# Opening attention's pool ahead of the layer norm's last steps, with its stores and key loads on GpSimd's queue, in a fused hybrid encoder layer

## The chip, the cores and the metric

The kernel runs on one core of one Trainium2 chip. The metric is the device time of one execution in microseconds (us). All times below are of the kernel before the change.

## The reference

One layer over 2048 tokens of width 1024, in float32, with a batch of one:

```python
mod = c_act @ w_ada + b_ada                       # adaptive norm
shift, scale, gate = split(mod, 3)
h = rmsnorm(x, norm_w) * (1 + scale) + shift
proj = h @ w_in + b_in                            # 1024 -> 4624 columns
na_q, na_k, na_v, na_z, ml_q, ml_k, ml_v, ml_o, ml_z, gates = split(proj)
na = neighbourhood_attention(na_q, na_k, na_v, rpb) * silu(na_z)
                                                  # 8 heads of 64, an 8 x 16 window on a 32 x 64 grid
mq, mk = split(silu(short_conv([ml_q, ml_k])))
hm = mlstm(mq, mk, ml_v, fwd gates) + flip(mlstm(flipped, bwd gates))   # 4 heads of 128
ml = layer_norm(hm * sigmoid(ml_o)) * ml_norm_w * silu(ml_z)
x = x + gate * (concat(na, ml) @ w_out)
out = rmsnorm(x) * final_norm_w
```

## The kernel before

Every product of activations and weights is done as three matmuls on high and low parts (`hhi`, `hlo`, `whi`, `wlo`) that add into one PSUM tile. The normalised input stays in SBUF, transposed, in four groups of 512 tokens (`hhi0` to `hhi3` and `hlo0` to `hlo3`).

**Phase 1** makes the values, gates, the mLSTM's queries and keys, the tables of the attention's bias and the output weights times the gate, and parks most of them in DRAM.

**Phase 1b** (from about 555 us) runs the mLSTM head by head: `ml_pass1` builds the states chunk by chunk, `ml_pass2` makes the outputs and their moments, and a queue of small closures (`normalise`, `turn`, `end`, store) finishes the layer norm a few steps behind. `close_step` pops these queues. The product `hm` times the output gate of each chunk is GpSimd's, and VectorE's `bn_stats` reads what it leaves. Between these small steps TensorE is fed from the generator `nq_gen`, which makes the remaining projections: mLSTM's gate (`mz`), attention's gate (`nz`), keys (`k`) and queries (`q`). `pump(n)` puts n of its matmuls into the program. A turn of `nq_gen` is one strip of 128 weight columns: `nq_load` reads it to a single buffer (`rawq`), `nq_split` makes `whi` on ScalarE and `wlo` on GpSimd, or on VectorE for the queries, and 24 matmuls go to each group of tokens. ScalarE copies the result to `qst` as the high part, VectorE makes the low part in the same tile, and both go to DRAM (`d_kna`, `d_qna`). For keys and queries these two stores wait in the list `late` until the next group's third step. There are two such tiles, used in turn.

When the groups 3 and 2 are no longer needed as inputs their buffers become the keys of the attention, `kk`: the second half of the tokens is read back by the 16 loads of `kk_jobs`, each queued by `job` inside `close_step`; the first half is written there directly.

**Phase 2** does the attention in 16 patches of 8 x 16 tokens, four units (pairs of heads) each. `slot(n)` is written out by hand (`manual_schedule`): scores of unit n (`stage_s`: queries `qhigh` and `qlow`, a bias table `tab`, VectorE adds and takes the minimum, ScalarE takes the exponential into `pbuf`), outputs of n-2, transposes of n-1, loads, and a number of pumped matmuls. The slots 0 to 4 pump what is left of the queries' projection, 22 matmuls a slot; the later ones pump the output projection.

**Between the two** stands the end of the mLSTM: after its last step a loop runs `close_step` and `pump(PUMP3)` until the norm's queues are empty, then the pools `ml` (SBUF) and `ms` (PSUM) close, and `phase2` opens its pool `p2` in their place. A tile of the new pool waits for the last use of the old tiles at its address. The last gate tile, `zt_last`, stands in the ring of the `ck` tiles of `ml`, and its store is the last thing that the old pool does.

SyncE's, ScalarE's and GpSimd's instruction streams each issue DMAs in their own order. The framework also keeps eight semaphores for the DMAs that SyncE and ScalarE issue and eight for those of GpSimd; a DMA waits until the one that last used its semaphore has landed.

Of the kernel before, what the change touches and what calls it, by code (L numbers as in the profile page):

```python
# [58 lines left out]
class Kernel:  # L59
# [780 lines left out]
    def nq_gen(self):  # L840
# [10 lines left out]
        for i, s, g in order:  # L851
# [6 lines left out]
            for k in range(KT):  # L858
                w1, w2 = whi[:, k, off : off + P], wlo[:, k, off : off + P]
                for n, (w, h) in enumerate(((w1, self.hhi), (w1, self.hlo), (w2, self.hhi))):  # L860
                    nc.tensor.matmul(patch_ps(ps) if patch else ps, w, self.htok(h, g, k, patch), start=(k == 0 and n == 0), stop=(k == KT - 1 and n == 2))  # L861
# [48 lines left out]
        while late:  # L910
            nc.scalar.dma_start(*late.pop(0))
# [15 lines left out]
    def phase1b(self, left, right):  # L927
        nc = self.nc
        mls = ExitStack()
        ml = self.pool(mls, "ml", bufs=1, side="right")  # L930
        pps, pss = ExitStack(), ExitStack()
        self.pp = self.pool(pps, "pp2", bufs=2, space=PSUM)
        self.ms = self.pool(pss, "ms", bufs=1, space=PSUM)
# [4 lines left out]
        self.perm = ml.tile([P, P], F32, name="perm")  # L938
# [10 lines left out]
        for j, (steps, cur) in enumerate(passes):  # L949
            nxt = passes[j + 1][1] if j + 1 < len(passes) else iter(())  # L950
            for i in range(steps):
                if i in (steps - 4, steps - 1):
                    next(nxt, None)
                next(cur)
        while self.norms or self.turns or self.ends or self.stores:
            self.close_step()
            self.pump(PUMP3)
        mls.close()
        pss.close()
        self.todo = []  # L960
        self.stacks = [pps, right, left]
# [5 lines left out]
    def kk_jobs(self):  # L967
# [77 lines left out]
    def ml_pass2(self, ml, h):  # L1045
# [11 lines left out]
        def load_z(gi):  # L1057
            while ("mz", h, gi) not in self.zdone:
                self.pump(1)
            if h == MH - 1 and gi == NG - 1:  # L1060
                t = ml.tile([P, 769], F32, tag="ck", bufs=4, name="zt_last")[:, :512].rearrange("p (a q) -> p a q", a=4)
            else:
                t = ml.tile([P, 4, CH], F32, tag="zt", bufs=1, name=f"zt_{h}_{gi}")
# [12 lines left out]
        def combine(c):  # L1076
# [23 lines left out]
            if c % 4 == 0:  # L1100
                hm[gi] = ml.tile([P, 4, CH], F32, tag="hm", bufs=2, name=f"hm_{h}_{gi}")
                mv[gi] = ml.tile([P, 4, 2], F32, tag="mv", bufs=2, name=f"mv_{h}_{gi}")
# [5 lines left out]
        def moments(c):  # L1108
            gi = c // 4
            b6 = ml.tile([P, 6], F32, tag="b6", bufs=2, name=f"b6_{h}_{c}")  # L1110
            nc.vector.bn_stats(b6, hm[gi][:, c % 4, :])
            nc.vector.bn_aggr(mv[gi][:, c % 4, :], b6)
            if c % 4 == 3:
                v = ml.tile([P, 4], F32, tag="var", bufs=2, name=f"var_{h}_{gi}")
                y = ml.tile([P, 4], F32, tag="rstd", bufs=2, name=f"rstd_{h}_{gi}")
                nc.vector.tensor_scalar(v, mv[gi][:, :, 1], EPS, None, ALU.add)
                self.rsqrt(ml, y, v, f"{h}_{gi}")
                mu = ml.tile([P, 4], F32, tag="mu", bufs=2, name=f"mu_{h}_{gi}")
# [38 lines left out]
        for c in range(NC):  # L1157
# [37 lines left out]
    def phase2(self):  # L1195
# [426 lines left out]
```

## Time and profile before

| | |
|---|---|
| Median of 3 runs | 1409.82 us (1407.24 to 1413.92) |
| Profiled execution | 1409.69 us, of which the span is 1407.8 us |
| TensorE busy | 1316.7 us, 94% of the span |
| VectorE, ScalarE, GpSimd busy | 834.7, 529.7, 284.5 us |
| Bytes of DMA | 264.73 MB, 188 GB/s in the mean |
| Mean granted TensorE clock | 0.983 |

The profile is of one execution. "busy" of TensorE has the pipelined ends of matmuls in it. A row of the timeline gives start and length in us, the engine, the line, the operation with its tiles, and in brackets the idle time just before it with what ended that. A name such as ACTq or SPq is an engine's issuing of a DMA; its length is that of the issue and not of the transfer. A row that ends in "x4" holds four instructions merged. The windows view gives the busy time of each engine in a stretch, then the granted TensorE clock and the busy share of the DMA engines.

### The profile page before, as it was taken

The page shows a single profiled execution, that of the slowest core. Times are in us where ns is not written, and L with a number is a line of the kernel's source. Part 1 is how long each engine was busy: PE and PEld are TensorE (multiplying, and loading weights), DVE is VectorE, ACT ScalarE, POOL GpSimd, SP SyncE. Part 2 cuts the span into 40 slices and gives each one's busy share as a digit, 9 for nine tenths or more (in the row PEclk, how much of TensorE's full clock was granted, in tenths as well). Part 3 has the DMA queues.
Part 4 walks back from the last instruction along what each step waited for, and adds up shares of the span by engine and source line. Part 5 has one row for each costly group of instructions (what it writes and reads, how often), then busy time and mean ns, then how long its engine had stood idle before and what let it go on. Part 6 is the DMA issues. An engine that isn't in the chain of part 4 may idle for free. (4 is left out here: it accounts for less than half of the span.)

```text
span 1407.8 us, 23381 instructions
## 1 busy us (share of the span) xinstructions
PE 1316.7 (94%) x8052; PEld 1127.7 (80%) x8052; DVE 834.7 (59%) x2565; ACT 529.7 (38%) x1131; POOL 284.5 (20%) x309
## 2 busy tenths in 40 slices
PE   3989998898999999999999998999989999999996
PEld 2889998888887787788878786788867888888885
DVE  6683423211355569156757777877637777777674
ACT  4642344523222323113323313323336555555551
POOL 4353221424101010001212002212112211112111
PEclk9999999999999999999999999999999999999998
DMA  9798448777467675555666777946598897776862
GB/s 319 225 297 202 121 125 213 190 184 204 117 116 208 143 186 163 161 166 150 196 190 212 238 225 214 232 127 180 145 275 223 197 222 169 197 192 173 190 159 75
DMA packets 273036, 264.73 MB, mean 188 GB/s; under 512 B 33498, under 2 KB 233818, under 8 KB 272918
## 3 DMA queue, kind: packets, MB, share of 16 engines
q1 hardware_dynamic: 181486, 187.17, 50.3%
q0 software_dynamic: 21408, 38.05, 11.0%
q10 hardware_dynamic: 70024, 38.02, 9.6%
q8 instruction: 64, 1.05, 0.3%
q14 instruction: 54, 0.44, 0.1%
HBM read 178.62 MB, written 92.72 MB: 193 GB/s over the span
## 5 line engine op out<-in xcount | busy, mean ns | idle before, releaser
L861 PE MATMUL pq<-hhi,whi_a 128*128 128x512 f32 x512 | 211.6, 413 | 0.8 <-ACT u L769 0.8
L861 PE MATMUL pq<-hhi,wlo_a 128*128 128x512 f32 x512 | 211.4, 413 | 0.3 <-DVE wlo_a L838 0.3
L861 PE MATMUL pq<-hlo,whi_a 128*128 128x512 f32 x512 | 211.3, 413 | 0.0
L1342 ACT ACTIVATE pbuf<-pbuf,mn 128x480 f32<-128x480 f32 (+5 forms) x128 | 76.4, 598 | 115.3 <-DVE mn L1341 108.9
L861 PEld LDWEIGHTS pq<-hhi,whi_a 128*128 128x128 f32 x512 | 98.3, 192 | 19.4 <-ACT u L769 1.2
L861 PEld LDWEIGHTS pq<-hhi,wlo_a 128*128 128x128 f32 x512 | 98.2, 192 | 19.0 <-DVE wlo_a L838 0.8
L861 PEld LDWEIGHTS pq<-hlo,whi_a 128*128 128x128 f32 x512 | 98.3, 192 | 17.9
L1341 DVE CUSTOM_DVE_ANT_0 pbuf<-pS,tab 128x480 f32<-128x480 f32 (+5 forms) x128 | 65.2, 541 | 37.3 <-DMA tab<-d_t 20.1
L1415 PE MATMUL y<-hhi,whi_a 128*128 128x512 f32 x256 | 84.7, 400 | 0.7 <-ACT whi_a L1388 0.7
L1415 PE MATMUL y<-hhi,wlo_a 128*128 128x512 f32 x256 | 84.3, 399 | 0.0
L835 POOL TENSOR_TENSOR wlo_a<-rawq,whi_a 128x1024 fp32r<-128x1024 f32 x20 | 48.3, 2417 | 167.0 <-ACT whi_a L834 52.4
L425 PE MATMUL pvo<-whi_b,hhi 128*128 128x256 f32 x256 | 74.7, 292 | 7.5 <-DVE stvo L495 7.5
L1106 POOL TENSOR_TENSOR hm<-hm,ck 128x128 f32<-128x128 f32 x64 | 26.4, 413 | 266.5 <-DVE hm L1105 190.7
L1087 ACT ACTIVATE num<-px,gtile 128x129 f32<-128x129 f32 x120 | 38.2, 364 | 96.8 <-PE px L1082 79.9
L426 PE MATMUL pvo<-wlo_b,hhi 128*128 128x256 f32 x256 | 73.7, 288 | 0.0
L427 PE MATMUL pvo<-whi_b,hlo 128*128 128x256 f32 x256 | 73.5, 287 | 0.0
L1014 DVE TENSOR_SCALAR wv<-kv,gtile 128x129 f32<-128x129 f32 x120 | 38.5, 328 | 58.4 <-PE dc L1030 30.4
L495 DVE TENSOR_TENSOR stvo<-pvo,brow 128x256 f32<-128x256 f32 x64 | 26.6, 421 | 73.4 <-PE pvo L427 59.5
L710 ACT ACTIVATE dec<-dec,gtile 128x128 f32<-128x128 f32 x128 | 42.1, 392 | 74.0 <-POOL dec L706 64.8
L460 DVE TENSOR_TENSOR stv<-pv,brow 128x256 f32<-128x256 f32 x32 | 12.5, 421 | 89.2 <-DMA d_vna<-stv 41.6
L1363 PE MATMUL pT<-ident,pbuf 128*128 128x128 f32 (+2 forms) x416 | 59.8, 283 | 2.8 <-DVE pbuf L1353 2.8
L1378 PE MATMUL pO<-pt,v 128*64 128x128 f32 (+3 forms) x832 | 61.0, 280 | 1.3 <-ACT pt L1365 0.8
(295 smaller groups left out, 3578.0 us busy)
## 6 DMA issues: line engine op xcount, KB each, us to landing
ck<-d_ck SPq DMA_DIRECT2D x64, 384.5 KB
kv<-d_ck SPq DMA_DIRECT2D x120, 128.5 KB
rawq<-in_w_main_dram SPq DMA_DIRECT2D x30, 512.0 KB
raw<-in_w_main_dram SPq DMA_DIRECT2D x20, 512.0 KB
d_ck<-stvo SPq DMA_DIRECT2D x16, 514.0 KB
x<-in_x_dram SPq DMA_DIRECT2D x16, 512.0 KB
wada<-in_w_ada_dram SPq DMA_DIRECT2D x32, 256.0 KB
dec<-d_mneg SPq DMA_DIRECT2D x32, 256.0 KB
```

Of the source, the lines that this page charges most:

```text
L425: nc.tensor.matmul(ps, lhi(k), rhi(k), start=(k == 0), stop=False)
L426: nc.tensor.matmul(ps, lhi(k), rlo(k), start=False, stop=False)
L427: nc.tensor.matmul(ps, llo(k), rhi(k), start=False, stop=(k == KT - 1))
L710: nc.scalar.activation(t[:, d, o, :], t[:, d, o, :], AF.Exp, bias=self.cols["g"][:, d, h, c : c + 1])
L835: nc.gpsimd.tensor_tensor(lo[:, :, cs], raw, hi[:, :, cs].bitcast(F32), ALU.subtract)
L861: nc.tensor.matmul(patch_ps(ps) if patch else ps, w, self.htok(h, g, k, patch), start=(k == 0 and n == 0), stop=(k == KT - 1 and n == 2))
L1014: nc.vector.tensor_scalar(wv, tiles[d, i][:, 128:257], self.cols["w"][:, d, h, c : c + 1], None, ALU.mult)
L1341: nc.vector.tensor_tensor_reduce(pt[:, :nk], ps, tabs[place[u]][j][:, :nk], 1.0, 3e38, ALU.add, ALU.min, mn)
L1342: nc.scalar.activation(pt[:, :nk], pt[:, :nk], AF.Exp, bias=mn, scale=-1.0, accum_out=sums[:, j : j + 1])
L1363: nc.tensor.transpose(ps[:cs, i, :], pts[j][:, i * cs : (i + 1) * cs], self.ident)
L1378: nc.tensor.matmul(po[j * HD : (j + 1) * HD, :], v[:n, h * HD : (h + 1) * HD], pt[j][:n, i, :], start=(i == 0), stop=(i == nch - 1))
L1415: nc.tensor.matmul(y, m[:, k, :], w[k][:, cs], start=(k == 4 and n == 0), stop=(k == 3 and n == 2))
```

## The change

Four things are done at once. The layer norm's closing tiles (`zt`, `hm`, `mv`, the moments, `perm`) get a pool of their own, `mle`, that lies outside `ml` and lives on through phase 2, so that `ml` closes before the closing loop. The loop itself moves to a method `close`, called from `phase2` after `p2` is open and the first loads of the attention stand in the program; the last `load_z` moves there too, and `zt_last` becomes a tile of `p2`. The PSUM pools of phase 2 still open after the loop. Small tiles of phase 2 and three of the four `pbuf` take the places of closed norm tiles in `mle`. The late stores of keys and queries go from ScalarE's queue to GpSimd's, the 16 key loads from SyncE's to GpSimd's, the first six `qlow` loads from SyncE's to GpSimd's, and four of the eight loads of output weights from GpSimd's to SyncE's.

```diff
@@ nq_gen (here and at its end)
                         while late:
-                            nc.scalar.dma_start(*late.pop(0))
+                            nc.gpsimd.dma_start(*late.pop(0))
@@ phase1b
+        self.mle = self.pool(right, "mle", bufs=1, side="right")
         mls = ExitStack()
         ml = self.pool(mls, "ml", bufs=1, side="right")
...
-        while self.norms or self.turns or self.ends or self.stores:
-            self.close_step()
-            self.pump(PUMP3)
         mls.close()
-        pss.close()
         self.todo = []
         self.stacks = [pps, right, left]
+
+    def close(self):
+
+        self.last_z()
+        while self.norms or self.turns or self.ends or self.stores:
+            self.close_step()
+            self.pump(PUMP3)
+        self.pss.close()
@@ kk_jobs
-            self.nc.sync.dma_start(self.kk[ct][row : row + HD, j * T + T // 2 : (j + 1) * T].bitcast(F32), src)
+            self.nc.gpsimd.dma_start(self.kk[ct][row : row + HD, j * T + T // 2 : (j + 1) * T].bitcast(F32), src)
@@ ml_pass2 (zt, hm, mv, b6, var, rstd, mu: ml becomes self.mle)
             if h == MH - 1 and gi == NG - 1:
-                t = ml.tile([P, 769], F32, tag="ck", bufs=4, name="zt_last")[:, :512].rearrange("p (a q) -> p a q", a=4)
+                t = self.p2.tile([P, 4, P], F32, tag="pt", bufs=2, name="zt_last")
...
-                if h == MH - 1:
-                    load_z(NG - 1)
+                self.last_z = lambda: load_z(NG - 1)
@@ phase2
-        p = self.pool(rgt, "p2", bufs=1, side="right")
-        pss = ExitStack()
-        pS = self.pool(pss, "pS", bufs=3, space=PSUM)
-        pT = self.pool(pss, "pT", bufs=2, space=PSUM)
-        pO = self.pool(pss, "pO", bufs=1, space=PSUM)
+        p = self.p2 = self.pool(rgt, "p2", bufs=1, side="right")
+        few = self.mle
...
-                nc.sync.dma_start(lo[js, j].bitcast(F32), self.d_qna[1, c0 // 2, b, js])
+                (nc.gpsimd if i < 3 else nc.sync).dma_start(lo[js, j].bitcast(F32), self.d_qna[1, c0 // 2, b, js])
...
-            nc.gpsimd.dma_start(wolo[k].bitcast(F32), self.d_wo[k])
+            (nc.gpsimd if k < 4 else nc.sync).dma_start(wolo[k].bitcast(F32), self.d_wo[k])
...
         for t in qlow:
             nc.gpsimd.memset(t.bitcast(F32), 0.0)
+        for i in (0, 1):
+            load_q(i)
+            for j in range(2):
+                load_tab(follows.pop(-1 - i), j) if j else load_tab(follows[-1 - i], j)
         load_v(b0)
         load_z(b0)
-        for i in range(2):
-            load_q(i)
-        for i in (0, 1):
-            for j in range(2):
-                load_tab(follows.pop(-1 - i), j) if j else load_tab(follows[-1 - i], j)
-        pbuf = [p.tile([P, 512], F32, name=f"pbuf{i}") for i in range(4)]
+        load_q(2)
+        self.close()
+        pss = ExitStack()
+        pS = self.pool(pss, "pS", bufs=3, space=PSUM)
+        pT = self.pool(pss, "pT", bufs=2, space=PSUM)
+        pO = self.pool(pss, "pO", bufs=1, space=PSUM)
+        pbuf = [few.tile([P, 512], F32, tag=tag, bufs=bufs, name=f"pbuf_{i}") for i, (tag, bufs) in enumerate((("hm", 2), ("hm", 2), ("zt", 1)))]
+        pbuf.append(p.tile([P, 512], F32, name="pbuf_3"))
         for t in pbuf:
             nc.vector.memset(t, 0.0)
-        load_q(2)
```

The lines of the changed kernel from `nq_gen` to `ml_pass2` keep or gain up to five in their numbers.

How the order moves, first on TensorE at the first scores of the attention. `pq_12_1` is the projection of query strip 12 for token group 1, `pq_14_1` that of strip 14, one turn earlier; `pS_0_0` are the first scores. Before:

```order
L861 MATMUL pq_12_1_10305<-hhi1_103,wlo_a_127 128x512
L861 MATMUL pq_12_1_10305<-hhi1_103,whi_a_126 128x512
L1335 MATMUL pS_0_0_10324<-hhi3_1093,qhigh0_10218 128x288
L1336 MATMUL pS_0_0_10324<-hhi3_1093,qlow0_10221 128x288
L1335 MATMUL pS_0_1_10327<-hhi3_1093,qhigh0_10218 128x288
L1336 MATMUL pS_0_1_10327<-hhi3_1093,qlow0_10221 128x288
L861 MATMUL pq_12_1_10305<-hlo1_106,whi_a_126 128x512
```

And after:

```order
L861 MATMUL pq_14_1_10274<-hhi1_103,whi_a_126 128x512
L861 MATMUL pq_14_1_10274<-hlo1_106,whi_a_126 128x512
L1336 MATMUL pS_0_0_10327<-hhi3_1093,qhigh0_10125 128x288
L1337 MATMUL pS_0_0_10327<-hhi3_1093,qlow0_10128 128x288
L1336 MATMUL pS_0_1_10330<-hhi3_1093,qhigh0_10125 128x288
L1337 MATMUL pS_0_1_10330<-hhi3_1093,qlow0_10128 128x288
L861 MATMUL pq_14_1_10274<-hhi1_103,wlo_a_127 128x512
```

The first scores now stand 35 matmuls of the projection earlier, behind two matmuls of strip 14 in place of 13 of strip 12. The scores of unit 1 and the first transposes stand where they stood, so 57 matmuls lie between the two units' scores where 22 lay.

On SyncE's queue at the same place (`rawq_25`, `rawq_26`, `rawq_27` are the weights of the strips 13, 14 and 12 of the queries). Before:

```order
L1052 DMA ck_3_15_9902<-d_ck_61 128x769
L826 DMA rawq_25_9973<-in_w_main_dram 128x8x128
L826 DMA rawq_26_10141<-in_w_main_dram 128x8x128
L826 DMA rawq_27_10184<-in_w_main_dram 128x8x128
L1251 DMA qhigh0_10218<-d_qna_65 64x2x256 x2
L1254 DMA qlow0_10221<-d_qna_65 64x256 x2
```

And after:

```order
L1057 DMA ck_3_15_9905<-d_ck_61 128x769
L826 DMA rawq_25_9976<-in_w_main_dram 128x8x128
L1252 DMA qhigh0_10125<-d_qna_65 64x2x256 x2
L1309 DMA tab00_10132<-d_t20_81 128x288
L1309 DMA tab01_10133<-d_t20_81 128x288
L1252 DMA qhigh1_10126<-d_qna_65 64x2x256 x2
L1309 DMA tab10_10134<-d_t20_81 128x288
L1309 DMA tab11_10135<-d_t20_81 128x288
L1252 DMA qhigh2_10127<-d_qna_65 64x2x256 x2
L826 DMA rawq_26_10185<-in_w_main_dram 128x8x128
L826 DMA rawq_27_10228<-in_w_main_dram 128x8x128
```

The ten loads of the attention stand ahead of the two last weight strips, behind which they stood.

On GpSimd in the third head's second pass (`hm` is the product with the output gate, `wlo_a` a weight split). Before:

```order
L1106 TENSOR_TENSOR hm_2_1_8356<-hm_2_1_8356,ck_2_4_8200 128x128
L835 TENSOR_TENSOR wlo_a_127<-rawq_16_8253,whi_a_126 128x8x128
L1106 TENSOR_TENSOR hm_2_1_8356<-hm_2_1_8356,ck_2_5_8242 128x128
L1106 TENSOR_TENSOR hm_2_1_8356<-hm_2_1_8356,ck_2_6_8286 128x128
L1106 TENSOR_TENSOR hm_2_1_8356<-hm_2_1_8356,ck_2_7_8330 128x128
```

And after:

```order
L1111 TENSOR_TENSOR hm_2_1_8359<-hm_2_1_8359,ck_2_4_8203 128x128
L864 DMA d_qna_65<-qst_13_2_8402 128x4x128 x2
L835 TENSOR_TENSOR wlo_a_127<-rawq_16_8256,whi_a_126 128x8x128
L980 DMA hlo3_1094<-d_kna_66 64x1024
L1111 TENSOR_TENSOR hm_2_1_8359<-hm_2_1_8359,ck_2_5_8245 128x128
L980 DMA hhi3_1093<-d_kna_66 64x1024 x2
L1111 TENSOR_TENSOR hm_2_1_8359<-hm_2_1_8359,ck_2_6_8289 128x128
L980 DMA hhi3_1093<-d_kna_66 64x1024
L864 DMA d_qna_65<-qst_15_3_8497 128x4x128 x2
L980 DMA hhi3_1093<-d_kna_66 64x1024
L1111 TENSOR_TENSOR hm_2_1_8359<-hm_2_1_8359,ck_2_7_8333 128x128
```

Stores and key loads now stand between the products of successive chunks, up to four DMAs ahead of one product.

More of the change, by code (lines that the diff above doesn't have):

```diff
@@ L910, in nq_gen @@
         while late:
-            nc.scalar.dma_start(*late.pop(0))
+            nc.gpsimd.dma_start(*late.pop(0))
     def pump(self, n):
@@ L937, in phase1b @@
         self.zdone = set()
-        self.perm = ml.tile([P, P], F32, name="perm")
+        self.perm = self.mle.tile([P, P], F32, name="perm")
         nc.vector.tensor_copy(self.perm.rearrange("p (a r k) -> p a r k", r=2, k=16), patch_order(self.ident))
@@ L954, in phase1b @@
                 next(cur)
+        mls.close()
+        self.todo = []
+        self.stacks = [pps, right, left]
+    def close(self):
+        self.last_z()
         while self.norms or self.turns or self.ends or self.stores:
@@ L1109, in moments @@
             gi = c // 4
-            b6 = ml.tile([P, 6], F32, tag="b6", bufs=2, name=f"b6_{h}_{c}")
+            b6 = self.mle.tile([P, 6], F32, tag="b6", bufs=2, name=f"b6_{h}_{c}")
             nc.vector.bn_stats(b6, hm[gi][:, c % 4, :])
@@ L1326, in stage_s @@
             pts = []
-            sums = p.tile([P, 2], F32, tag="sums", bufs=3, name=f"sums_{u}")
+            sums = few.tile([P, 2], F32, tag="sums", bufs=3, name=f"sums_{u}")
             scores = []
@@ L1426, in outproj @@
             done.append(b)
-            rst = p.tile([P, 1], F32, tag="rst", bufs=2, name=f"frs_{b}")
-            var = p.tile([P, 1], F32, tag="var", bufs=2, name=f"fvar_{b}")
+            rst = few.tile([P, 1], F32, tag="rst", bufs=2, name=f"frs_{b}")
+            var = few.tile([P, 1], F32, tag="fvar", bufs=2, name=f"fvar_{b}")
             pr, pc = divmod(b, 4)
```

27 lines of the change are left out of this document (12 added, 15 removed).

## The prediction

> **What bounds the kernel now.** I read the page first, then what TensorE waits for, stretch by stretch, then the timelines of the engines that it waits for.
>
> ```profile
> PE 1316.7 (94%) x8052; PEld 1127.7 (80%) x8052; DVE 834.7 (59%) x2565; ACT 529.7 (38%) x1131; POOL 284.5 (20%) x309
> ```
>
> TensorE is busy 94% of the span; no other engine is above 60%, and the change leaves the number of matmuls as it was. So the change can only take away, or add, time in which TensorE stands still or runs on a lowered clock. The waits of TensorE in the two stretches that the change touches, the mLSTM (560 to 1000 us) and the passage into the attention (1012 to 1064 us):
>
> ```profile
> PE dc L1030 <- DVE wv L1014: 7.0, 7, 2.1
> PE px L1082 <- ACT num L1087: 3.3, 2, 3.0
> PE px L1082 <- DVE st L1040: 2.1, 2, 1.1
> PE pi L1084 <- DVE num L1089: 1.6, 1, 1.6
> PE ht L1139 <- ACT hm L1131: 1.5, 1, 1.5
> PE a L1069 <- DMA ck<-d_ck: 1.4, 1, 1.4
> ...
> PE pT L1363 <- DVE pbuf L1353: 2.8, 1, 2.8
> PE pS L1335 <- DVE mn L1341: 2.2, 1, 2.2
> PE pS L1336 <- DMA qlow<-d_qna: 1.1, 1, 1.1
> PE pq L861 <- DVE wlo_a L838: 0.3, 1, 0.3
> ```
>
> The first six are 16.9 us over 440 us, the last four 6.4 us within some 15 us. The passage has a second price, the clock:
>
> ```profile
> 1037.57 1.52 PE L1363 MATMUL pT<-ident,pbuf 128*96 128x128 f32 x6 [2.79 <-DVE pbuf L1353]
> 1038.74 0.78 PE L861 MATMUL pq<-hhi,wlo_a 128*128 128x512 f32 x1
> ...
> 1043.58 0.41 PE L861 MATMUL pq<-hlo,whi_a 128*128 128x512 f32 x1
> 1043.82 0.39 PE L861 MATMUL pq<-hhi,wlo_a 128*128 128x512 f32 x1
> ...
> 1047.62 0.86 PE L1363 MATMUL pT<-ident,pbuf 128*96 128x128 f32 x6
> ...
> 1040.00:1044.00 4.00, 4.00 (x11) 3.10 (x11) 0.10 (x2) 0.19 (x1) 0.00 (x0) 0.55 1.14 245
> ```
>
> After the waits the granted clock (the last column but two) is 0.55. From 1038.74 to 1043.58 us there are 11 matmuls, 0.44 us apart; right after it they start 0.24 us apart. That is 11 x 0.20 = 2.2 us lost, and the six transposes take 1.52 for 0.86 us, 0.7 more. **The passage costs 6.4 + 2.9 = 9.3 us.** Why TensorE waits there:
>
> ```profile
> 1002.49 0.41 POOL L1106 TENSOR_TENSOR hm<-hm,ck 128x128 f32<-128x128 f32 x1 [2.93 <-DVE hm L1105]
> 1017.98 1.46 POOL L1454 MEMSET qlow<- 128x512 f32 x3 [15.07 <-DMA d_mix<-zt_last]
> ...
> 1005.18 0.54 SPq L826 DMA_DIRECT2D rawq<-in_w_main_dram  x1
> ...
> 1012.31 0.54 SPq L826 DMA_DIRECT2D rawq<-in_w_main_dram  x1
> 1017.96 1.27 SPq L1251 DMA_DIRECT2D qhigh<-d_qna  x2
> ...
> 1024.14 6.62 SPq L1308 DMA_DIRECT2D tab<-d_t  x4
> ...
> 1033.73 0.46 DVE L1341 CUSTOM_DVE_ANT_0 pbuf<-pS,tab 128x288 f32<-128x288 f32 x1 [11.11 <-DMA tab<-d_t]
> ```
>
> The last large tile of the old pool is free at 1002.9 us. But everything that goes to the new pool starts at 1018, when the store of `zt_last` has landed. The tables are issued from 1024.1, and VectorE stands idle for 11.1 us until the first of them lets it add the bias at 1033.7.
>
> **The change, part by part.**
>
> *The earlier pool* removes the cause. `zt_last` isn't in the old pool any more, so the ten loads on SyncE and the fills and loads on GpSimd can start at about 1003 in place of 1018. The first scores move 35 matmuls (8.3 us) forward, to about 1015.8 (strip 13's end, by the copy at 1015.29 below, and two matmuls), and 57 matmuls (13.5 us) lie between them and the next unit's, where 22 (5.2 us) lay. With the tables landed by 1015, bias, exponential and scaling (from 1033.73 to the transposes at 1037.57, 4 us) end some 9 us before TensorE wants `pbuf`. All three waits on `qlow`, `mn` and `pbuf` should go, and the low clock with them: **-9.3 us**, if nothing else is late.
>
> What is late next is the weight strip `rawq_26`. It stood ahead of the ten loads and was issued at 1005.18; now it stands behind them.
>
> ```profile
> L1251 SPq DMA_DIRECT2D qhigh<-d_qna x35: 599/606/2622, 1018.0 to 1345.6; - x35
> L1308 SPq DMA_DIRECT2D tab<-d_t x8: 319/323/2117, 1024.1 to 1044.5; - x8
> 1017.61 1.06 ACT L837 ACTIVATE whi_a<-rawq 128x1024 fp32r<-128x1024 f32 x1 [1.63 <-DMA rawq<-in_w_main_dram]
> 1015.29 0.69 ACT L898 ACTIVATE qst<-pq,bcol 128x512 fp32r<-128x512 f32 x1 [4.27 <-PE pq L861]
> L838 DVE SCALAR_TENSOR_TENSOR wlo_a<-rawq,whi_a x4: 1212/1224/1226, 988.3 to 1020.5; 128x1024 fp32r<-128x1024 f32 x4
> ```
>
> Six `qhigh` of 0.606 and four `tab` of 0.323 take SyncE 4.9 us, so it issues `rawq_26` at 1008 at the earliest, 1010 if it waits for a semaphore. A strip took 5.3 us from issue to use (1012.31 to 1017.61); beside 2 MB of new loads I take up to 6. It lands between 1013.3 and 1016, its high part is ready 1.06 later, and TensorE wants it at 1015.2 (strip 13's end, by the copy at 1015.29): 0 to 1.9 us late. The next strip's chain is 5.3 + 1.06 + 1.22 = 7.6 us, against 24 matmuls and four scores, 6.2 us: 1.4 us late. Then a strip has two groups and the chain catches up. `zt_last` is loaded 10 us later than it was, and 2 transposes may wait for VectorE behind it: up to 1 us. I take **+3.0 us**, the middle of 0.3 (its wait now) and 6. I count no low clock for waits this short, because the one of 2.2 us is still followed by one of 2.8 before the clock falls.
>
> *Key loads and stores leave SyncE and ScalarE.* What they cost there, at the worst place:
>
> ```profile
> 860.65 0.37 ACTq L1149 DMA_DIRECT2D d_mix<-zt  x1
> ...
> 871.05 0.37 ACTq L1064 DMA_DIRECT2D zt<-d_zml  x1
> 871.51 0.69 ACT L898 ACTIVATE qst<-pq,bcol 128x512 fp32r<-128x512 f32 x1 [9.21 <-DMA hlo<-d_kna]
> ...
> 874.11 0.71 PE L1082 MATMUL px<-st,ck 128*128 128x129 f32 x4 [2.97 <-ACT num L1087]
> 876.38 1.23 PE L1084 MATMUL pi<-ck 128*128 128x129 f32 x4 [1.55 <-DVE num L1089]
> ```
>
> ScalarE stands 9.2 us behind one load of `zt`, which waits for a key load's semaphore and for a store that was queued behind two of `d_qna`; TensorE loses 1.4 + 3.0 + 1.6 = 6.0 us to it (with the wait for `ck`). The change takes both away from ScalarE, but not the bytes: the DMA engines are full there (1.09 in the row at 856 below). I take half, **-3.0 us**, between 0 and -6.
>
> The Trainium skill ("DMA: Bandwidth & Descriptors", Issuing engines are not separate DMA queues) speaks against this: DMAs of all issuing engines share the same 16 engines, so another issuer only saves issue time. By that rule this term is 0 and the sum 3 us higher; the row agrees on the shared engines, but a wait that names the key load is more than issue time.
>
> *GpSimd's queue takes them.* Each store waits there for ScalarE's or VectorE's part of `qst`, and behind it stand the product `hm` and now and then a weight split `wlo_a`. In the mLSTM these are 8 pairs of key stores, 8 pairs of query stores and 16 key loads.
>
> ```profile
> 856.00:860.00 4.00, 4.00 (x25) 3.44 (x24) 2.88 (x12) 0.96 (x3) 0.41 (x1) 1.00 1.09 341
> sum 104.00, PE 94.16 PEld 78.46 DVE 82.40 ACT 33.80 POOL 20.04; mean PE 3.62 PEld 3.02 DVE 3.17 ACT 1.30 POOL 0.77
> L1311 POOL DMA_DIRECT2D hlo<-d_wo x8: 527/544/651, 1023.1 to 1067.8; - x8
> L1271 POOL DMA_DIRECT2D v<-d_vna x40: 626/680/907, 1019.4 to 1347.3; - x40
> DVE b L1111 <- POOL hm L1106: 4.7, 11, 0.5
> v<-d_vna POOLq DMA_DIRECT2D x16, 256.0 KB, 9.4
> ```
>
> GpSimd's issues cost 0.54 to 0.68 us, 0.91 at most. So 48 DMAs are some 30 us of an engine that is idle 80% of the time; what counts is the product `hm` queued behind them, for which VectorE already waits at `b` (4.7 us in 11 waits from 790 to 935). A pair delays it by 1.1 to 1.4 us, a key load by 0.5 to 0.7. VectorE has 104 - 82.4 = 21.6 us free in 840 to 944, nearly 1 us in each step of 4.3, so most is absorbed. I take **+2.0 us** for the steps where two delays meet. The lower bound is 0; for the upper, a query store has four pieces a partition where these rows have one, and at four times 0.54 it would take 2.2 us: that is a rival below. The output weights that go to SyncE wait there for TensorE's last use of `hlo1`, with `rawq_30` behind them, which is wanted three groups later: 0.
>
> The split is wanted a turn later, so it costs nothing. ScalarE fills a `qst` tile again two groups later, 48 matmuls or 11.4 us at 0.24, more in the mLSTM; GpSimd's transfers of this size land 9.4 us after their issue (the last row), so the tile is just free: 0, but with ScalarE's later exponentials behind it if it isn't.
>
> **The sum**: -9.3 + 3.0 - 3.0 + 2.0 = -7.3 us, against the profiled 1409.69 us: **1402.4 us**. The profiled time is the median (1409.82) to 0.1 us, so I take it for the median too.
>
> **The rivals.**
>
> *A. GpSimd's stores hold up the norm (slower).* If a query store takes 2.2 us to issue, a pair holds `hm` up by 4.4 us every two steps. VectorE's spare is some 2 us in that time, and TensorE waits behind VectorE for the other 2.4: 8 x 2.4 = 19 us in place of the 2, so 1409.7 - 7.3 + 17 = **1419 us**. It turns slower than before from an issue of about 1.7 us. For it: no row has this shape, and the order has up to four DMAs ahead of one product. Against it: `d_wo` with 4 KB a partition costs no more than `d_vna` with 2 KB.
>
> The Trainium skill ("SBUF — State Buffer", A bandwidth-pool intuition that's wrong) has another way to it: GpSimd's descriptor writing starves while VectorE holds the shared port, 620 ns becoming 3100. By that figure a pair would take 6.2 us and the sum go past 1430, as an estimate from that page; the 40 issues above, spread from 1019 to 1347 us over VectorE's work, never passed 907 ns.
>
> *B. The strips take back the passage (no change).* If SyncE's ten loads wait for semaphores and land as slowly as in the trace (1024.14 to 1033.73), `rawq_26` is some 4 us late and `rawq_27` 2, together 6 us with 2.2 us of low clock, and the mLSTM brings nothing: -9.3 + 8.2 + 0 + 1 = **1409.6 us**. For it: the DMA engines are full whenever these loads run.
>
> *C. Both stalls go whole (faster).* -9.3 + 0.3 - 6.0 + 0 = **1394.7 us**.
>
> **The numbers.** Forecast 0.40, A 0.20, B 0.25, C 0.15. About 0.5% (7 us, 1402.7) is what a measurement of this kernel can tell from no change. The forecast stands at that line; its own spread (1398 to 1406, from the strips' 0 to 6) I count 0.30 faster and 0.10 the same. C is faster, B the same, A slower: faster 0.45, same 0.35, slower 0.20. The range reaches from C to A, **1394 to 1418**, and leaves out the worse half of A and what C may exceed.
>
> **What would show it.** Right: `qlow` filled at about 1003; no wait of `pS` or `pT` in the passage and a granted clock of 1.00 there; a wait of `pq` on `whi_a` or `wlo_a` of 1 to 4 us before strip 14 or 12; ScalarE's 9.2 us at 862 to 871 shortened; query stores on GpSimd of 0.5 to 1.2 us each. Wrong: such stores above 1.7 us with VectorE's wait at `b` growing by 10 us or more (A); waits of `pq` above 5 us in the passage (B); or a new wait elsewhere, such as ScalarE's `qst` waiting for a store that GpSimd issued late.

## The result and the profile after

The changed kernel takes 1419.78 us (median of 5 runs, 1418.54 to 1421.13), the kernel before 1409.82 (also of 5): a ratio of 1.0076, 95% interval 1.0048 to 1.0105. It is slower by 0.76%; the forecast was 1402.4 us and faster, and the time lies above the range of 1394 to 1418. The profiled execution took 1419.59 us with a span of 1417.5, and is compared here with the one of before (1409.69 and 1407.8).

The first line of the page is the busy time of the engines. TensorE has the same work (1317.9 us), GpSimd 43 us more; it is still idle 77% of the time.

```profile
PE 1317.9 (93%) x8052; PEld 1130.0 (80%) x8052; DVE 833.4 (59%) x2565; ACT 528.8 (37%) x1131; POOL 327.8 (23%) x375
```

Cut by TensorE's own work (the first matmul after its wait for `u` at 557, the last group of `pi`, the first `y`, the end of the last matmul), the timelines give three stretches, in us:

| | mLSTM | passage | attention |
|---|---|---|---|
| before | 442.3 | 70.9 | 324.6 |
| after | 445.0 | 73.1 | 330.6 |
| after less before | +2.7 | +2.2 | +6.0 |
| the prediction | -1.0 | -6.3 | 0 |

**The passage.** What the prediction removed is gone. `qlow` is filled at 1005.29, and in the waits of PE from 1003 to 1100 us no `pS` and no `pT` is left. In their place stands one wait of 9.5 us:

```profile
PE pq L861 <- ACT whi_a L837: 9.5, 1, 9.5
PE pO L1379 <- DVE sums L1352: 3.8, 1, 3.8
...
PE pq L861 <- DVE wlo_a L838: 0.9, 2, 0.5
```

The timeline (start, duration, engine) shows how the weight strip `rawq_26` came to be that late (strips are called by their `rawq` number from here on):

```profile
1005.26 1.28 SPq L1252 DMA_DIRECT2D qhigh<-d_qna  x2
1005.29 1.46 POOL L1455 MEMSET qlow<- 128x512 f32 x3
1006.87 1.06 ACT L837 ACTIVATE whi_a<-rawq 128x1024 fp32r<-128x1024 f32 x1 [0.44 <-DVE var L1121]
...
1010.20 0.48 DVE L1471 MEMSET pbuf<- 128x512 f32 x1 [0.99 <-DMA d_mix<-zt]
1010.62 1.22 DVE L838 SCALAR_TENSOR_TENSOR wlo_a<-rawq,whi_a 128x1024 fp32r<-128x1024 f32 x1
1010.94 2.04 SPq L1252 DMA_DIRECT2D qhigh<-d_qna  x2
1013.08 0.60 SPq L826 DMA_DIRECT2D rawq<-in_w_main_dram  x1
1026.28 1.06 ACT L837 ACTIVATE whi_a<-rawq 128x1024 fp32r<-128x1024 f32 x1 [12.49 <-DMA rawq<-in_w_main_dram]
1027.39 0.79 PE L861 MATMUL pq<-hhi,whi_a 128*128 128x512 f32 x1 [9.54 <-ACT whi_a L837]
```

It is issued at 1013.08, for two reasons that end within 1.1 us of each other. The later one is SyncE, which is at its tenth load until 1012.98. The other is the strip's one buffer, which is free only when VectorE has split strip 25, at 1011.84: VectorE had a part of the layer norm and fills of `pbuf` ahead of it, one of which waits for the store of `zt`, whose tile `pbuf` now reuses. In the timeline of the kernel before, VectorE split that strip right behind ScalarE:

```profile
1002.64 1.06 ACT L837 ACTIVATE whi_a<-rawq 128x1024 fp32r<-128x1024 f32 x1 [2.17 <-PE pq L861]
1003.92 1.23 DVE L838 SCALAR_TENSOR_TENSOR wlo_a<-rawq,whi_a 128x1024 fp32r<-128x1024 f32 x1
```

After its issue the strip takes 13.2 us to its use; in the kernel before one took 5.3. The windows say why (the columns from the end: GB/s, DMA share, granted clock):

```profile
1008.00:1012.00 4.00, 3.47 (x16) 2.43 (x15) 2.77 (x12) 0.69 (x1) 3.40 (x6) 1.00 1.12 335
1012.00:1016.00 4.00, 4.00 (x19) 3.08 (x20) 2.56 (x7) 1.65 (x4) 2.62 (x4) 1.00 1.05 204
1016.00:1020.00 4.00, 1.85 (x8) 1.14 (x6) 0.00 (x0) 0.00 (x0) 0.00 (x0) 1.00 1.12 198
1020.00:1024.00 4.00, 0.00 (x0) 0.00 (x0) 0.00 (x0) 0.00 (x0) 0.00 (x0) 0.53 1.03 296
1024.00:1028.00 4.00, 0.61 (x2) 0.51 (x3) 0.63 (x1) 1.70 (x3) 0.00 (x0) 0.50 0.26 77
1028.00:1032.00 4.00, 4.00 (x15) 3.39 (x14) 2.89 (x9) 2.37 (x5) 1.50 (x2) 0.69 0.64 174
```

The DMA engines are full (a share of 1.03 to 1.12) for 16 us and move some 4.1 MB in them. From 1018 to 1026 all engines of the core stand still, the granted clock falls to 0.53 and 0.50, and the first nine matmuls after the stand lose another 1.5 us (they take 3.2 us, and 1.7 at the spacing of full clock).

**The attention.** In slot 6 TensorE waits 3.8 us where it waited 0.5, and its next twelve `pO` take 1.55 us, for 0.88 six us later; the granted clock is 0.57 from 1088 to 1092. VectorE waits for `gtile`, which GpSimd now loads behind two query stores (the timeline). The load is issued 2.7 us after the first `y`, before 1.0, and lands 10.2 us after its issue, before 7.7:

```profile
1075.02 0.77 POOL L911 DMA_DIRECT2D d_qna<-qst  x1 [2.36 <-ACT qst L898]
1076.56 0.77 POOL L911 DMA_DIRECT2D d_qna<-qst  x1 [0.78 <-DVE qst L899]
...
1077.99 0.58 POOL L1282 DMA_DIRECT2D gtile<-d_zna  x1
...
1088.28 0.29 DVE L1381 TENSOR_TENSOR gtile<-pO,gtile 128x128 f32<-128x128 f32 x1 [7.06 <-DMA gtile<-d_zna]
1088.72 1.55 PE L1379 MATMUL pO<-pt,v 120*64 120x128 f32 x12 [3.78 <-DVE sums L1352]
```

**The mLSTM.** ScalarE's stand at 862 to 872 is still there, though neither stores nor key loads are on its queue or SyncE's any more (the timeline of ACT). The store of `zt` is issued at 861.17, 0.5 us after its old time, and the reload follows 11.0 us later; before, it was 10.4.

```profile
861.17 0.41 ACTq L1154 DMA_DIRECT2D d_mix<-zt  x1
...
872.14 0.37 ACTq L1069 DMA_DIRECT2D zt<-d_zml  x1
872.64 0.69 ACT L898 ACTIVATE qst<-pq,bcol 128x512 fp32r<-128x512 f32 x1 [9.93 <-DMA d_mix<-zt]
```

GpSimd's new DMAs, by line (the second number after the bar is the mean in ns of one issue):

```profile
L864 POOL DMA_DIRECT2D d_qna<-qst x30 | 23.0, 767 | 77.2 <-ACT qst L898 61.1 <-issue 7.4 <-DVE qst L899 5.0
L864 POOL DMA_DIRECT2D d_kna<-qst x16 | 9.2, 577 | 13.5 <-ACT qst L898 10.2 <-DVE rstd L1196 1.9 <-DVE hm L1110 0.6
L980 POOL DMA_DIRECT2D hhi<-d_kna x8 | 4.4, 547 | 0.1
```

A query store costs GpSimd 0.77 us to issue, a key store or key load 0.55 to 0.58. VectorE's wait for GpSimd's product (the waits of DVE from 540 to 1000 us) is no longer than before, when it was 14.7 us in 35 waits:

```profile
DVE b L1116 <- POOL hm L1111: 13.4, 34, 2.4
```

### The profile page after: what moved, and what is told of

It reads as the page before. It is cut to its first block, busy times and chain, and to the rows that moved or that the text cites. A ratio compares the mean times of both kernels' runs of the same rounds, so it can differ in the third digit from the quotient of the medians.

```text
span 1417.5 us, 23429 instructions
## 1 busy us (share of the span) xinstructions
PE 1317.9 (93%) x8052; PEld 1130.0 (80%) x8052; DVE 833.4 (59%) x2565; ACT 528.8 (37%) x1131; POOL 327.8 (23%) x375
## 5 line engine op out<-in xcount | busy, mean ns | idle before, releaser
L1379 PEld LDWEIGHTS pO<-pt,v 128*64 128x64 f32 (+3 forms) x832 | 45.2, 138 | 22.8 <-issue 15.5
```

What stands on the lines that cost most here:

```text
L1379: nc.tensor.matmul(po[j * HD : (j + 1) * HD, :], v[:n, h * HD : (h + 1) * HD], pt[j][:n, i, :], start=(i == 0), stop=(i == nch - 1))
```

## The experiments

The ratios are to the kernel before on the same chip; the chips differ by some 1% in their times, so times of different chips are not compared. Traces are of one execution each. Two of the changed kernel differ by 2.3, 1.9 and 0.5 us in the three stretches; in the six traces of kernels that are the same up to the end of the mLSTM, this stretch takes 445.0 to 450.9 us; and the work ahead of the mLSTM, which no edit touches, differs by up to 6.1 us on one chip. So a single trace is read for its waits, and a stretch only where several traces agree.

**Is it the strip's place in SyncE's queue, or the full DMA engines?** First, the strip on another queue, and then the ten loads:

```
-        nc.sync.dma_start(raw, self.w_main[...])
+        (nc.scalar if i == 26 else nc.sync).dma_start(raw, self.w_main[...])
```

> Only the issuer of one transfer changes: the weight strip rawq_26 is issued by ScalarE in place of SyncE, so the ten attention loads no longer stand ahead of it. Theory 1 (the place in SyncE's queue is the cause): it is issued at about 1005 us, lands in 5 to 7 us, TensorE's wait of 9.5 us for whi_a and most of the 0.5 clock after it go, and the kernel takes 1408 to 1411 us, 9 to 12 less than the changed kernel's 1419.8. Theory 2 (the ten loads fill the DMA engines, whatever the queue): it is issued early too but lands with the ten loads at 1018 us or later, the wait stays at 3 us or more, and the time is 1413 us or more. Theory 3 (the strip is a symptom and something else is late at the same point, zt_last or the first scores): a wait of the same size under another name, 1417 to 1420.

Ratio 1.0076 (1.0046 to 1.0107). ScalarE issues the strip at 1005.95, 7.4 us after the first of the ten loads, and it is used at 1017.87; TensorE waits 8.2 us. The issue is hardly earlier than the 7.8 us of the changed kernel: VectorE empties the strip's buffer only at 1004.75 here. But no load of the attention stands ahead of it on ScalarE's queue, and it is still under way for 11.9 us.

```profile
1005.95 0.69 ACTq L826 DMA_DIRECT2D rawq<-in_w_main_dram  x1
1017.87 1.06 ACT L837 ACTIVATE whi_a<-rawq 128x1024 fp32r<-128x1024 f32 x1 [9.53 <-DMA rawq<-in_w_main_dram]
```

```
-                nc.sync.dma_start(hi[rows]..., src)
+                (nc.gpsimd if i < 3 else nc.sync).dma_start(hi[rows]..., src)
-            nc.sync.dma_start(tabs[place[u]][j]...)
+            (nc.gpsimd if u < 3 else nc.sync).dma_start(tabs[place[u]][j]...)
```

> The strip stays on SyncE; six qhigh and four table loads of the first units are issued by GpSimd, before and between qlow and v. Theory 1 (order on SyncE): the same gain as with the strip on ScalarE, 1408 to 1411 us, less about 1 if v and zs come late for the first outputs. Theory 2 (the DMA engines are full): the wait for the strip shrinks by no more than half, 1413 to 1417. GpSimd has ten more issues of 0.55 us ahead of v (5.5 us): the first d_qna stores behind them come that much later, and if qst is reused before they land, ScalarE waits there and gives back 1 to 3 us.

Ratio 1.0077 (1.0052 to 1.0103). With SyncE's queue empty, strip 26 takes 6.1 us, issued 4.4 us after the first load, and strip 27, eight us deeper in the burst, 9.5 (the timeline of SyncE and ScalarE); the waits for the high parts are 1.2 and 5.1 us. The place in the queue alone (theory 1) falls: a strip is late on any queue while the burst lasts.

```profile
1006.11 0.55 SPq L826 DMA_DIRECT2D rawq<-in_w_main_dram  x1
1012.17 1.06 ACT L837 ACTIVATE whi_a<-rawq 128x1024 fp32r<-128x1024 f32 x1 [3.97 <-DMA rawq<-in_w_main_dram]
1014.51 0.54 SPq L826 DMA_DIRECT2D rawq<-in_w_main_dram  x1
1024.03 1.06 ACT L837 ACTIVATE whi_a<-rawq 128x1024 fp32r<-128x1024 f32 x1 [10.23 <-DMA rawq<-in_w_main_dram]
```

**What do the queue moves cost?** One part taken back from the changed kernel, then the pool's move alone, with the changed kernel beside it as a yardstick:

```
e3:  -nc.gpsimd.dma_start(*late.pop(0))      +nc.scalar.dma_start(*late.pop(0))        (both places)
e4:  -self.nc.gpsimd.dma_start(self.kk[ct]   +self.nc.sync.dma_start(self.kk[ct]
e7:  e3 and e4, qlow on nc.sync, all of load_w on nc.gpsimd
```

> The key and query stores go back to ScalarE's queue; all else is the changed kernel. If the stores on GpSimd cost time (gtile<-d_zna issued 6 us later with a TensorE wait of 3.8 us and 1.5 of low clock in slot 6, and the mLSTM's last hm 2.3 us later): 1412 to 1415 us. If they took a wait off ScalarE, as the prediction has it (3 us for stores and key loads together): 1420 to 1423. If the two cancel: 1418 to 1421, with ScalarE's 9 us stand at 862 back and no stall in slot 6.

> The sixteen key loads go back to SyncE's queue; all else is the changed kernel. If it is only the issuer that changes while the DMA engines are the limit: 1419 to 1421 us, no change. If the key loads on GpSimd hold up the product hm: 1416 to 1418. If they relieved SyncE and ScalarE by half of the prediction's 3 us: 1421 to 1423.

> The changed kernel itself, as a yardstick on the chip of the other three. Its ratio to the kernel before was 1.0076 (1.0048 to 1.0105); 1.005 to 1.0105 is expected again, with TensorE's wait for the strip at 8 to 11 us and a stall of 3 to 4 us at pO in slot 6.

> The pool's move alone: key and query stores on ScalarE, key loads and query low halves on SyncE, output weights on GpSimd, as before the change. If the queue moves cost time (the mLSTM 3 to 4 us longer, slot 6's stall with its low clock 5 us): 7 to 9 us under the changed kernel, ratio to the kernel before 1.001 to 1.003, and the strip's wait still 9 to 11 us. If the queue moves took 3 us off ScalarE as predicted: 3 us above the changed kernel, ratio 1.009 to 1.011. Stretches: the mLSTM from the first strip's group to the last pi back at 441 to 443 us (445 in the changed kernel), no stall over 1 us at pO in slot 6.

And the other way round, on the kernel before, both queue moves and each alone:

> The kernel before with only its stores of keys and queries and its key loads on GpSimd's queue; the pools as before. The runs so far (changed kernel 1.0085, pool's move alone 1.0018) put the queue moves at 0.67% or 9.4 us. If that is theirs alone: ratio 1.004 to 1.008, the mLSTM 3 to 6 us longer and the stall of 3 to 4 us at pO in slot 6 there. If the queues cost only together with the earlier pool: 0.999 to 1.002. If they gain 3 us as predicted: 0.998.

> The kernel before with only its key and query stores on GpSimd's queue. Both queue moves together cost 1.1% (0.9 to 1.3) there. If the stores are the larger part (they stand in front of gtile and hm on GpSimd): 1.006 to 1.010, with a stall of 2 to 4 us at pO in slot 6 and the mLSTM 3 to 6 us longer. If the key loads are: 1.000 to 1.004, the mLSTM within 2 us of before.

> The kernel before with only its sixteen key loads on GpSimd's queue. If they cost by being let go together (eight in 9 us in place of 15, so that the store of zt lands after 11 us in place of 7 to 10, with its reload and ScalarE behind it): 1.003 to 1.007, the mLSTM 2 to 5 us longer, no stall in slot 6. If only the stores cost: 0.998 to 1.002. If it frees SyncE as predicted: 0.997 to 0.999.

| kernel | ratio to before | mLSTM | passage | attention |
|---|---|---|---|---|
| changed, again | 1.0085 (1.0068 to 1.0102) | 447.3 | 71.2 | 330.1 |
| changed, stores back | 1.0058 (1.0032 to 1.0084) | 442.8 | 74.8 | 323.9 |
| changed, key loads back | 1.0047 (1.0025 to 1.0069) | 441.0 | 71.7 | 328.9 |
| pool's move alone | 1.0018 (1.0003 to 1.0032) | 436.4 | 75.3 | 326.4 |
| before, both queue moves | 1.0108 (1.0091 to 1.0126) | 450.3 | 69.3 | 327.8 |
| before, stores alone | 1.0045 (1.0027 to 1.0063) | 442.2 | 70.2 | 328.8 |
| before, key loads alone | 1.0056 (1.0034 to 1.0079) | 443.9 | 71.6 | 324.3 |

The queue moves cost the time. On the kernel before, stores alone cost 0.45% and key loads alone 0.56%; together they cost 1.1%. On the changed kernel the two taken back give 0.27% and 0.38%, but against a changed kernel on another chip, whose interval theirs overlap (the second's barely). The pool's move alone, on the same chip, stands 0.67% below the changed kernel. So the stores or the key loads on GpSimd cost some 4 to 8 us each, and the pool's move by itself brings nothing: in its trace the passage is 4.4 us longer than before, with a wait of 12.7 us for the strip. The stores' cost shows in the attention: it takes 327.8 to 330.6 us in the eight traces with all of them on GpSimd, 323.4 to 327.3 in the eight with all on ScalarE. The mLSTM takes 445 to 451 us with both on GpSimd (seven traces), 441 to 444 with one (four). With none it is 442 in the old pool (two) and 436 to 440 with the earlier pool (five). That both together lengthen the mLSTM is shown. Where the 0.56% of the key loads alone lies is not: their trace is of the fastest of six runs, 6.0 us under the median, and its three stretches are only 2.0 us longer than those before. With both moves, the waits that grow in the mLSTM (from the waits of PE) are those behind ScalarE, while the one for `wv` falls.

```profile
PE px L1082 <- ACT num L1087: 7.4, 2, 4.3
PE dc L1030 <- DVE wv L1014: 5.4, 4, 2.4
PE ht L1139 <- ACT hm L1131: 3.7, 2, 2.2
```

These are of both queue moves on the kernel before; without the moves they were 3.3, 7.0 and 1.5. The store of `zt` and its reload are 11.3 us apart, against 10.4 before, 11.0 after and 6.7 with the pool's move alone, so ScalarE's stand goes with how soon that store lands, and was as long with an empty queue as with a full one. The next store of `zt`, some 25 us later, does the same: its reload follows after 11.3 us, before 5.8 (the timeline of ACT, both queue moves on the kernel before):

```profile
887.31 0.37 ACTq L1064 DMA_DIRECT2D zt<-d_zml  x1
887.72 0.68 ACT L881 ACTIVATE hhi<-pq,bcol 64x512 fp32r<-64x512 f32 x1 [8.08 <-DMA d_mix<-zt]
```

The two gaps sum to 17.7 to 23.3 us in the seven traces with both moves and to 11.6 to 16.2 in the seven with none, and over all 18 traces the mLSTM is longer where the sum is larger (a correlation of 0.93). So this is where the mLSTM's time goes as far as the traces tell; no run changes these landings alone. In the earlier pool with the old queues the first gap is 6.3 to 9.7 us, in the old pool 9.4 and 10.4; why it tends to be shorter stays open (the timeline of ACT, pool's move alone):

```profile
852.96 0.37 ACTq L1154 DMA_DIRECT2D d_mix<-zt  x1
859.64 0.37 ACTq L1069 DMA_DIRECT2D zt<-d_zml  x1
```

**Which store makes the stall in slot 6?** One pair, the one at the end of the generator, back on ScalarE:

```
         while late:
-            nc.gpsimd.dma_start(*late.pop(0))
+            nc.scalar.dma_start(*late.pop(0))
```

> The changed kernel with one pair of its stores, the last query group's at L911, back on ScalarE. All kernels with that pair on GpSimd so far stalled at pO in slot 6 by 2.7 to 7.0 us; those with it on ScalarE by 0 to 2. If that pair delays the load of gtile behind it: the stall falls from 3.8 to under 1.5 us, the part from the first output projection to the end from 330.5 to 324 to 327 us, the ratio to the kernel before from 1.008 to 1.004 to 1.006. If all the stores on GpSimd do it together: the stall stays at 3 us or more, ratio 1.007 to 1.010.

The stall at `pO` is gone (1.0 us in two waits), the attention takes 326.5 us. But ScalarE now issues the pair ahead of the split of the mixed rows, and TensorE waits 3.1 us there. The ratio is 1.0083 (1.0052 to 1.0115): the wait has changed its place, and no gain is shown.

```profile
PE y L1416 <- ACT whi_a L1389: 3.1, 1, 3.1
PE pO L1379 <- ACT pt L1366: 1.0, 2, 0.7
```

**Can the passage be had with fewer bytes in flight?** The other loads moved into slots 0 and 1, then with the old queues too, then with a gate: a copy of one column that makes GpSimd wait for a strip before it lets its loads go.

```
-        for i in (0, 1): load_q(i); ... tables
-        load_v(b0); load_z(b0); load_q(2)
+        load_q(0); ... tables
-            0: [lambda: nc.sync.dma_start(zs[1], ...)], 1: [...]
+            0: [load_v(b0), load_q(1), load_z(b0), ...], 1: [load_q(2), ...]
```

```
+        def gate(): nc.gpsimd.tensor_copy(t, self.wslot[0][0][:, 0, P : P + 1]...)
-            0: [load_v(b0), load_q(1), load_z(b0), ...], 1: [load_q(2), ...]
+            0: [gate, load_v(b0), load_q(1), load_z(b0), ...], 1: [load_q(2), ...]
```

> Only unit 0's query and the two units' tables are loaded at the pool's opening; the queries of units 2 to 5, v and zs are issued in slots 0 and 1, behind the strips. Theory 2 (what is in flight on the shared DMA engines sets the strip's landing): the bytes in front of rawq_26 fall from some 3.3 to 1.5 MB, it lands within 5 to 8 us of its issue, TensorE's wait for whi_a falls from 9.5 to 0 to 4 us and the low clock with it: ratio to the kernel before 0.997 to 1.002, some 0.7% under the changed kernel. Rival (the strip's place in the queue behind at least some loads): six loads still stand ahead of it, so the wait only falls to 6 to 7 us. Risk: v or zs late for the first output in slot 2, a wait at pO L1379 of 1 to 3 us.

> Both cures: fewer loads at the pool's opening, and the stores back on ScalarE, the key loads back on SyncE. If the two costs are separate and add: the passage's stalls gone, mLSTM and slot 6 as before the change: 6 to 10 us under the kernel before, ratio 0.993 to 0.996, about where the prediction put the change. If the passage's time comes back elsewhere (the strip, zt_last or v late): 0.998 to 1.001.

> As the kernel with fewer loads and the old queues, but GpSimd waits for the high part of strip 27 (one copy of 128x1) before it issues v, qlow of units 2 to 5 and zs, 1.2 MB. So about 1.6 MB in place of 2.8 is in flight when rawq_26 is issued. Theory 2 (the strip lands when the burst has drained, whatever its place): it lands 5 to 8 us after its issue in place of 13.2, TensorE's wait falls from 8.4 to 0 to 3 us, the low clock after it goes, and the ratio to the kernel before falls from 0.998 to 0.992 to 0.995. Rival 1 (the strip's own transfer or a semaphore is slow in this place): landing stays at 10 us or more, ratio 0.998. Rival 2 (v and zs come too late): a wait of 2 to 5 us at pO in slot 2, ratio 0.996 to 1.000.

Without the gate GpSimd issues `v` and `zs` at once all the same, and only some 0.5 MB had left the burst: ratios 1.0068 (1.0050 to 1.0085) and 0.9983 (0.9966 to 1.0000), the strip was still 10.2 and 13.3 us under way, TensorE's waits 5.3 and 8.4 us. Behind the gate the strip takes 5.7 us (the timeline), and TensorE waits 0.8 for it:

```profile
993.39 0.57 SPq L826 DMA_DIRECT2D rawq<-in_w_main_dram  x1
999.08 1.06 ACT L837 ACTIVATE whi_a<-rawq 128x1024 fp32r<-128x1024 f32 x1 [3.77 <-DMA rawq<-in_w_main_dram]
```

The same first load, nearly the same issue of the strip, fewer bytes (us from the first `qhigh` to the strip's issue, and to its use):

| kernel | to the issue | to the use |
|---|---|---|
| changed; again | 7.8; 7.8 | 21.0; 19.9 |
| strip by ScalarE | 7.4 | 19.3 |
| stores back; key loads back | 7.2; 7.5 | 22.3; 20.4 |
| pool's move alone | 16.6 | 24.3 |
| fewer loads; with old queues | 6.5; 6.3 | 16.7; 19.6 |
| gated; two gates; gate and order | 6.1; 6.5; 6.3 | 11.8; 12.1; 11.0 |

So theory 2 holds: the strip lands when what is in flight has drained. A strip that was issued 9 us later (the pool's move alone) landed only some 4 us later. There the place in the queue did count as well: the buffer was free at 998.39, and SyncE was at the attention's loads until 1008.70. But the gated kernel's ratio is 0.9984 (0.9960 to 1.0009), no better than without the gate: its waits of 3.4 us for `whi_a` at `y` and 2.2 for `qhigh` at `pS` have come in. Two attempts at these, with GpSimd issuing `qhigh` of units 2 to 5 in both. The first has a gate for each strip and the last pair of stores on GpSimd; the second has one gate, another order and the last pair a slot later on ScalarE:

```
e12: +  0: [gate(0), load_v(b0), gate(1), load_q(1), load_z(b0), ...]
     +  while late: nc.gpsimd.dma_start(*late.pop(0))
e15: +  0: [gate, load_q(1), load_v(b0), load_z(b0), ...]
     -  while late: nc.scalar.dma_start(*late.pop(0))
     +  self.last = late
     +  5: [nc.scalar.dma_start(*a) for a in self.last], load_z(b1)
```

> As the gated kernel, but v is let go after strip 26's high part, the queries of units 2 to 5 and zs after strip 27's, those queries by GpSimd and not behind the tables on SyncE, and the last pair of query stores (3.4 us on ScalarE there, with the out projection's first weights behind it) by GpSimd. If the gated kernel's two remaining stalls (2.2 us at pS for qhigh, 3.4 us at y for whi_a) hang on these two: both go, and the ratio to the kernel before falls from 0.998 to 0.993 to 0.996. If the engines' load only moves the wait to another transfer: 0.997 to 1.000.

> The gated kernel (one gate, behind strip 27) with two edits: the queries of units 2 to 5 are issued by GpSimd, right behind the gate and ahead of v, and the last pair of query stores is issued by ScalarE a slot later, behind the split of the mixed rows. If the gated kernel's two stalls (2.2 us at pS for qhigh, 3.4 us at y for whi_a) hang on these: both go, no stall over 2 us from the passage on, ratio to the kernel before 0.993 to 0.997. If v, now behind the queries, is late instead: a wait of 1 to 4 us at pO in slot 2 and 0.997 to 1.000.

The first gives 1.0012 (0.9995 to 1.0029): `v` beside strip 27 makes that one late by 5.6 us, and the pair ahead of `gtile` brings slot 6's stall back, longer:

```profile
PE pO L1379 <- DVE sums L1352: 7.0, 1, 7.0
PE pq L861 <- ACT whi_a L837: 6.4, 2, 5.6
```

The second has no wait over 1.3 us from the passage on in its trace, and a passage of 65.9 us, 5.0 below before (that is the prediction's -6.3, nearly). Its ratio is 0.9982 (0.9961 to 1.0004). Three versions lie at 0.998, and none is shown to beat the kernel before.

**The tables first.** The kernel before, with the four tables ahead of the later queries:

```
-        load_v(b0); load_z(b0); load_q(0); load_q(1); ... tables
+        load_q(0); ... tables; load_q(1); load_v(b0); load_z(b0)
```

> The kernel before with the four tables issued right behind the first unit's queries, ahead of those of the later units; nothing else. The passage's waits for mn (2.2 us) and pbuf (2.8 us) and 2.9 us of low clock hang on the tables, issued from 1024.1 and landed at 1033. If the order in SyncE's queue decides, they land 4 to 6 us earlier and 5 to 8 us go: ratio 0.994 to 0.997. If they land when the burst has drained, whatever their place: 0.998 to 1.001.

Ratio 1.0054 (1.0030 to 1.0077): slower. The tables do come early (VectorE's first bias 9.0 us after the first `qhigh`'s issue, 15.8 before), and the wait for `mn` goes. But ScalarE stands 12 us ahead of a query store's issue, with the copy of `pT` behind it (the timeline of ACT), and TensorE waits 7.8 us for that copy (the waits of PE). By the trace's semaphore records the issue waits for the semaphore of a query store that ScalarE issued at 1016.98 (the second of the first row below), and that store lands at 1032.36:

```profile
1012.84 4.51 ACTq L864 DMA_DIRECT2D d_qna<-qst  x2
1019.78 0.67 ACT L898 ACTIVATE qst<-pq,bcol 128x512 fp32r<-128x512 f32 x1
1032.44 0.93 ACTq L864 DMA_DIRECT2D d_qna<-qst  x2
1033.41 0.54 ACT L1342 ACTIVATE pbuf<-pbuf,mn 128x288 f32<-128x288 f32 x1 [12.97 <-issue]
```

```profile
PE pO L1378 <- ACT pt L1365: 8.6, 2, 7.8
```

## Why the prediction was wrong, point by point

The three stretches together are 18.2 us longer than forecast: the passage 8.5, the attention 6.0, the mLSTM 3.7. The two steps that failed most are the strip and GpSimd's queue.

- **The earlier pool, -9.3.** Right: the three waits went, with `qlow` filled 12.7 us earlier. They stay away in the kernel with one gate and another order too, where no late strip hides them.
- **The strip, +3.0 (0.3 to 6): the step that failed in the passage.** Its mechanism was named, and both its figures were too small. "1008 at the earliest, 1010" became 1013.08. The first load was issued at 1005.26 in place of 1003, because the mLSTM ended 2.3 us later, and the ten loads took SyncE 7.7 us in place of 4.9: the step took median issues, though the prediction's own row has four tables at 6.62 us. It also left out the strip's one buffer and the engine that empties it, VectorE, which the change had given `pbuf` to fill; that alone would have held the strip until 1011.84. "Up to 6 us" became 13.2, because the step took the landing of a strip from a stretch where the DMA engines were not full (a share of 0.5 to 0.8); the prediction's row for the tables (9.6 us under such a burst) was nearer. "I count no low clock" fell with it. The term is 9.5 + 0.9 (the waits for `wlo_a`) + 1.5 (low clock) = 11.9 us. With the -9.3 that makes the passage 2.6 us longer in place of 6.3 shorter; measured are 2.2.
- **Key loads and stores off ScalarE, -3.0 (0 to -6).** It came to nothing: the stand is 9.93 us after 9.21, and TensorE's waits in the mLSTM sum to 17.5 us after 16.9. The step took the key load that the row names for the cause; it was the store of `zt` and its reload. By the Trainium skill ("DMA: Bandwidth & Descriptors", Issuing engines are not separate DMA queues) this term was 0, and the stand in the trace agrees with it. The runs go further the other way: changing only the issuer cost 0.45% and 0.56%.
- **GpSimd's queue, +2.0, and the attention at 0: the other step that failed.** The place was wrong. `hm` was not held up (13.4 us of waits at `b` after 14.7). What was left out is the load of `gtile` behind the last pair of stores, in the attention, which the prediction held unchanged: +6.0 us there, of which some 4 go with that pair alone. Per move, the runs give 0.45% for the stores and 0.56% for the key loads, some 6 to 8 us each. For the stores most of it is in the attention; for the key loads the cause stays open, beyond the later landing of `zt`.
- **The zeros.** The output weights on SyncE showed no wait that names them.
- **Rival A** has the right time (1419 us) by luck, by the wrong way: 0.77 us a store, far from its 1.7, and the wait at `b` did not grow. The rise to 3100 ns that the Trainium skill ("SBUF — State Buffer", A bandwidth-pool intuition that's wrong) states did not show: the longest query store took 824 ns.
- **Rival B** named the mechanism, and its sign for a wait above 5 us came. Its 8.2 us were too little, the strip cost 11.9; and it had nothing for the attention.

## What to carry to other kernels

When a buffer comes free earlier, everything that waited for it starts at once: price each transfer behind that by its landing in the fullest stretch of the trace, not in a quiet one, and let go first what the next engine needs. A transfer's issue is the later of its queue and its buffer, so look up who empties the buffer and what the change puts ahead of that. Stores moved to an idle engine's queue cost little in issue time, but they stand ahead of that engine's own next load, and that is where to look.

## What the runs showed of the hardware

- A weight strip of 512 KB was used 4.8 to 5.3 us after its issue in the kernel before, where the DMA engines were busy 0.5 to 0.8, and 10 to 15 us after it behind a burst, whether SyncE or ScalarE issued it; full DMA engines moved between 198 and 335 GB/s in the windows above.
- ScalarE stood 12 us ahead of a query store's issue in one trace (1020.5 to 1032.4), until a store issued 15 us before had landed.
- TensorE had no work from 1017.9 to 1027.4. Its granted clock was 1.00 up to 1020, 0.53 from 1020 to 1024, 0.50 to 1028, and 0.69 in the four us from 1028, in which it worked again.
